# Layer 0: the order of key products, modulation steps and the first w_out loads

## The chip, the cores and the metric

One core of a Trainium2 chip runs the whole kernel. The metric is the device time of one execution in microseconds. The time before is 2219.7 us, the median of three runs (2218.09 to 2219.76).

## The reference, cut to what matters

A two-layer encoder trunk on 256 tokens of width 2048. Each layer computes six modulation vectors from a condition vector `c`, one input projection for four parallel mixers, one output projection, and a gated feed-forward network with a short convolution.

```python
for l in range(DEPTH):                                   # 2 layers
    mod = (c_act @ w_mod[l] + b_mod[l]).reshape(bn, 6, d)   # shift, scale, gate, twice
    h = layer_norm(x) * (1.0 + scale_m) + shift_m
    uv, q_c, kv_c, k_r, sb, sc, sh, ag = jnp.split(h @ w_in[l], IN_SPLITS, axis=-1)
    y_a = gmlp_mixer(uv, ...)
    y_b = mla_mixer(q_c, kv_c, k_r, ...)                  # latent attention with rotary key
    y_c = short_conv_mixer(sb, sc, sh, sconv_w[l])        # sb * conv3(sc * sh)
    y_d = conformer_conv(ag, ...)                         # 31 taps, layer norm, silu
    y = jnp.concatenate([y_a, y_b, y_c, y_d], axis=-1) @ w_out[l]
    x = layer_norm(ALPHA * x + (1.0 + gate_m) * y, ...)
    ...                                                   # shift_f, scale_f, gate_f: conv_ffn
```

In `mla_mixer` the key latent `kv_c` (256 columns) is RMS-normalised and scaled by a gain; the rotary key `k_r` (64 columns) is `k_r * cos + rotated(k_r) * sin`. All of this is float32.

## The kernel before, in words

The weights are larger than the on-chip memory, so they stream through it, issued by SyncE's queue (SP) in program order. A *unit* is one load of a group's weights and the products on it: for a width of 1024 columns, two blocks of 128 rows. `stream` loads a unit, then emits the products of the unit before it, then `pump`s modulation steps at the rate of the phase, then some background steps (the conformer's taps among them).

In layer 0 the weights of w_in are multiplied as they are, in float32 (tile `wexact`, 512 KB per block of 128 rows and 1024 columns; L374). Those tiles take turns through two sets of four buffers. Most other weights go through `wraw` (1 MB; L379) and are split into two halves: ScalarE casts `whi` (L390), VectorE subtracts for `wlo` (L391). In w_out of layer 0 the first two units (`PLAIN_UNITS`) of the first 1024 columns are exact, the next six are split, and the last 1024 columns are exact.

The modulation runs on VectorE beside all of this. Each step takes a 1 MB load (`wmod`) into one of four `raw` buffers and makes one pass of 128x2048 over it. For a gate (`gate_steps`, L295, L205) sixteen steps add up in one accumulator, `macc`, and a bias row follows (L298, L301). For a shift or scale (`column_steps`, `mod_block`, L193, L194) each step gives one column. `mods` is the stream of all these steps, and `next(mods, None)` emits one.

Layer 0 runs its groups in the order of `by_blocks`: the products that need only the first blocks, then the latent group B (`B_w`, `B_n`), whose result starts attention, then the short conv's group C (1024 columns, eight units, two of them loaded ahead), and then w_out.

When B's products are done, `mix_b` loads the attention weights, emits `MODS_AHEAD` = 3 modulation steps and remembers the last of them in `stepped`. It copies the latents out of PSUM (`lat`), and `attend` goes on:

- TensorE transposes the latents into `ps_q` and `ps_kv` (`turn`, L1073); these PSUM tiles (`ms_tile`) are two buffers that all of attention shares, so each new one waits until the one before the last has been read.
- ScalarE scales the query latents (`qg`, L1079, L1082).
- VectorE makes the key's products with cos and sin (`kc`, L1085, L1086) and scales the key latents (`kvr`, L1090). `behind` puts L1085 and L1090 after the step in `stepped` on VectorE's queue. That is an order at build time, without a semaphore.
- TensorE multiplies `kc` by two constant matrices (`ps_kr`), and ScalarE copies the result into `rope` (L1098, L1099). The conformer's scaled taps on ScalarE (`scaled`, L876) stand behind these copies; VectorE adds each tap to `convD` (L879).
- TensorE makes `ps_qn`, `ps_qr`, `ps_kn`, `ps_v` from the latents and the attention weights, and so on to the softmax and its products.

The order of instructions on each engine is fixed when the program is built, by a list scheduler: an instruction that comes earlier in the program goes first, and a later one fills in where the earlier is expected to wait.

Of the kernel before, what the change touches and what calls it, by code (L numbers as in the profile page):

```python
# [9 lines left out]
AF = mybir.ActivationFunctionType  # L10
ALU = mybir.AluOpType
# [4 lines left out]
S = 256  # L16
# [9 lines left out]
C_UV, C_Q, C_SB, C_SC, C_AG = 0, 1024, 1728, 2240, 3264  # L26
# [13 lines left out]
STEPS = [  # L40
    dict(B=1, C=6, out=2, up=2),
    dict(U=7, B=4, C=4, E=8, out=0, up=2),
]

PLAIN_UNITS = 2

MODS_AHEAD = 3

BATCHES = ((0, 4), (4, 4), (8, 4), (12, 4))

# [36 lines left out]
def encoder_kernel(ctx: ExitStack, tc: tile.TileContext, A: dict, consts: bass.AP, out: bass.AP):  # L87
    nc = tc.nc
    pe, act, dve, pool = nc.tensor, nc.scalar, nc.vector, nc.gpsimd
# [41 lines left out]
    sinT = cst[:, 768:1024]  # L131
# [50 lines left out]


    MOD = {}
    last_step = [None]
    data_dep = mybir.DependencyInfo(mybir.DependencyClass.Sync, mybir.DependencyReason.DATA)
    order_dep = mybir.DependencyInfo(mybir.DependencyClass.NoSync, mybir.DependencyReason.DATA)

# [11 lines left out]
    def mod_step(acc, w, kt, first):  # L200
        col = cact[:, kt : kt + 1]
        if first:
            i = dve.tensor_scalar(out=acc, in0=w, scalar1=col, scalar2=None, op0=ALU.mult)
        else:
            i = dve.scalar_tensor_tensor(out=acc, in0=w, scalar=col, in1=acc, op0=ALU.mult, op1=ALU.add)  # L205
        held(i, "mod")
        last_step[0] = i.ins.name

    def gate_rows(l, m, acc):

# [115 lines left out]


    pending = []
    postponed = []
    background = []  # L330

# [28 lines left out]
    def weights(w, k0, nk, c0, width, exact=False, spare=0):  # L360

        w, l = w
        n = nk * width
        if exact:
            parts, per = [], min(nk, max(1, 1024 // width))
            for k in range(0, nk, per):
                if spare:
                    r = slot("wexact")
                else:
                    tag = ("whi", "wlo")[exact_turn[0] % 2]  # L370
                    exact_turn[0] += 1
                    r = splitp.tile([P, 1024], F32, tag=tag, name="wexact")
                m = per * width
                nc.sync.dma_start(out=r[:, :m], in_=w.take(m, rows_of(l, k0 + k, per, c0, width)))  # L374
                for j in range(per):
                    parts.append((r[:, j * width : (j + 1) * width], None))
            return parts
        raw = raw_tile("wraw")
        nc.sync.dma_start(out=raw[:, :n], in_=w.take(n, rows_of(l, k0, nk, c0, width)))  # L379
        per = max(1, 1024 // width)  # L380
        parts = []
        for k in range(0, nk, per):
            m = per * width
            if k < spare:
                hi, lo = slot("thi", F32R), slot("tlo", F32R)
            else:
                hi = splitp.tile([P, 1024], F32R, tag="whi", name="whi")
                lo = splitp.tile([P, 1024], F32R, tag="wlo", name="wlo")
            r = raw[:, k * width : k * width + m]
            held(act.copy(hi[:, :m], r), "cast")  # L390
            i = dve.tensor_tensor(out=lo[:, :m], in0=r, in1=hi[:, :m].bitcast(F32), op=ALU.subtract)  # L391
            held(i, "split")
            for j in range(per):
                parts.append((hi[:, j * width : (j + 1) * width], lo[:, j * width : (j + 1) * width]))
        return parts
# [148 lines left out]
        for u in range(KT // 4):  # L544
            pump()

    def run(g, ahead=0):
        units, load, products, end, bg = g
        loaded = []

        def get(u):
            while len(loaded) < min(u + 1 + (ahead if u > 0 else 0), units):
                loaded.append(load(len(loaded)))
            return loaded[u]

        for u in range(units):
            stream(lambda: get(u), lambda item, u=u: products(item, u), bg)
            pending.extend(postponed)
            postponed.clear()
        pending.append(end)  # L560
# [46 lines left out]
    def out_proj(l, stage, w, src, order, gate_of, name, post_g, post_b, before, then, plain=(), bg=0):  # L607
# [112 lines left out]
        for c0, width in CHUNKS:  # L720
            last = c0 + width == D
            nk = 2048 // width
            units = nkt // nk
            state = {"tail": []}

            def load(u, c0=c0, width=width, nk=nk, units=units, last=last):
                item = load_unit(u, c0, width, nk, units, last)
                if last and u == units - 1:
                    gains()
                return item  # L730

            def load_unit(u, c0, width, nk, units, last):
                kt = order[nk * u]
                assert order[nk * u : nk * u + nk] == list(range(kt, kt + nk))
                spare = nk if last and units - 4 <= u < units - 2 else 0
                exact = c0 in plain or (bool(plain) and u < PLAIN_UNITS)
                parts = weights(w, kt, nk, c0, width, exact, spare)
                s4 = src(kt // 4)
                if exact:
                    return parts, [(s4[:, kt % 4 + k, :], None) for k in range(nk)]  # L740
                acts = []
                for k in range(0, nk, 2):
                    pair = kept.get(kt + k)
                    if pair is None:
                        pair = act_pair("a")
                        split(pair, s4[:, kt % 4 + k : kt % 4 + k + 2, :])
                        if nkt == KT:
                            kept[kt + k] = pair
                    for j in range(2):
                        acts.append([h[:, j, :] for h in pair[:2]])  # L750
                return parts, acts

            def unit(item, u, state=state, c0=c0, width=width, nk=nk, last=last, units=units):
                if u == 0:
                    state["ps"] = [
                        [acc_tile(f"{name}_{c0}{t}{i}") for i in range(width // 512)] for t in range(2)
                    ]
                if last and u >= units - 4:
                    state["tail"].append((item, u))
                    return  # L760
                for t in range(2):
                    products(t, item, state["ps"], u, nk)

            if c0 > 0:
                phase(l, f"{stage}_last" if last else f"{stage}_next")
            for u in range(units):
                stream(lambda: load(u), lambda item, u=u, unit=unit: unit(item, u), bg if c0 == 0 else 1)

            def done(state=state, c0=c0, nk=nk, last=last):
                if c0 == 0:  # L770
                    box["gate"] = gate_of()
                for t in range(2):
                    for item, u in state["tail"]:
                        products(t, item, state["ps"], u, nk)
                    if t == 0 and last and before is not None:
                        before()
                if last:
                    drain_background()
                elif c0 == 0:
                    background.append(lambda: None)  # L780
                for t in range(2):
                    for i, p in enumerate(state["ps"][t]):
                        q = c0 // 512 + i
                        if last:
                            finish(t, p, q)
                        else:
                            background.append(lambda t=t, p=p, q=q: finish(t, p, q))
                    if last:
                        norm(t)
                if last:  # L790
                    closed.append(True)

            pending.append(done)


    def mixers(l, w_in, Y, hF=None, first_mod=None, quarter=None):
# [265 lines left out]
        def attend(WQ, WKV, lat, q01, rr):  # L1062
# [3 lines left out]
            def behind(i):  # L1066
                if stepped:
                    tc.add_manual_dep(i.ins, stepped[0], order_dep, reason="these steps' weights land before the latents turn")
# [14 lines left out]
            by = turn(ps, S, [lat[t][:, 256:320] for t in range(2)])  # L1083
            kc = tmp_tile("kc")
            behind(dve.tensor_tensor(out=kc[0:64, 0:S], in0=by[0:64, :], in1=cosT[0:64, :], op=ALU.mult))  # L1085
            dve.tensor_tensor(out=kc[0:64, S : 2 * S], in0=by[0:64, :], in1=sinT[0:64, :], op=ALU.mult)  # L1086
            ps = ms_tile("ps_kv")
            for j in range(2):
                by = turn(ps, j * S, [lat[t][:, j * P : (j + 1) * P] for t in range(2)])
                behind(dve.tensor_scalar(out=kvr[:, j, :], in0=by, scalar1=KVG(j), scalar2=None, op0=ALU.mult))  # L1090

            rope = slot("rope").rearrange("p (j s) -> p j s", j=4)
            ps = ms_tile("ps_kr")
# [211 lines left out]
    def by_blocks(l, w_in, hF, first_mod, quarter, mix_d, mix_u, gelu_v, mix_v, mix_b, mix_c, mix_e):  # L1305
# [94 lines left out]
            mix_c(cps, tps)  # L1400
            mix_e(sumE, None)

        run(group(w_in, C_SC, 1024, f"C{l}", mix_ce, hF=hf, bg=STEPS[l]["C"]), 2)


    def ffn_up(l, G):
# [280 lines left out]
```

## Time and profile before

| | before |
|---|---|
| median of three runs | 2219.7 us |
| profiled execution, its own time | 2218.06 us |
| its span, first to last instruction | 2216.3 us |
| TensorE busy | 2192.1 us (99%) |
| VectorE busy | 1716.9 us (77%) |
| ScalarE busy | 1092.7 us (49%) |
| DMA, mean over the span | 273 GB/s |

The profile gives, for one execution, the busy time of each engine, groups of instructions by line, and timelines. In a timeline row stand the start in microseconds from the span's beginning, the time taken, the engine, the line of the kernel, the operation, the tile written and the tiles read, the shape and the count of merged instructions, and in brackets the idle time just before and what ended it. SPq is SyncE's queue, where a row is the issue of a transfer. In a row of a stretch stand its bounds, its length, the busy time and count of each engine, the granted TensorE clock, the busy share of the DMA engines and GB/s.

### The profile page before, as it was taken

The page shows a single profiled execution, that of the slowest core. Times are in us where ns is not written, and L with a number is a line of the kernel's source. Part 1 is how long each engine was busy: PE and PEld are TensorE (multiplying, and loading weights), DVE is VectorE, ACT ScalarE, POOL GpSimd, SP SyncE. Part 2 cuts the span into 40 slices and gives each one's busy share as a digit, 9 for nine tenths or more (in the row PEclk, how much of TensorE's full clock was granted, in tenths as well). Part 3 has the DMA queues.
Part 4 walks back from the last instruction along what each step waited for, and adds up shares of the span by engine and source line. Part 5 has one row for each costly group of instructions (what it writes and reads, how often), then busy time and mean ns, then how long its engine had stood idle before and what let it go on. Part 6 is the DMA issues. An engine that isn't in the chain of part 4 may idle for free. (4 is left out here: it accounts for less than half of the span.)

```text
span 2216.3 us, 28397 instructions
## 1 busy us (share of the span) xinstructions
PE 2192.1 (99%) x10880; PEld 1801.1 (81%) x10880; DVE 1716.9 (77%) x2209; ACT 1092.7 (49%) x1677; POOL 21.9 (1%) x38
## 2 busy tenths in 40 slices
PE   9999999999999999999999999999999999999997
PEld 6776875588888888888867988868888888888886
DVE  5658996799888888989968988877766656565776
ACT  3132740655555545545665555465455545454453
POOL 0000000000000000000000000000000000000000
PEclk9999999999999999999999999999999999999999
DMA  9999889588888888888758547856755555555553
GB/s 393 417 374 390 338 330 391 224 331 316 327 315 322 325 328 316 319 329 323 282 208 297 186 156 263 320 197 247 265 210 188 182 198 190 190 190 190 192 192 148
DMA packets 94034, 603.96 MB, mean 273 GB/s; under 512 B 10565, under 2 KB 10693, under 8 KB 29125
## 3 DMA queue, kind: packets, MB, share of 16 engines
q1 hardware_dynamic: 93898, 602.15, 74.0%
q8 instruction: 85, 1.39, 0.2%
q14 instruction: 51, 0.42, 0.1%
HBM read 600.01 MB, written 2.10 MB: 272 GB/s over the span
## 5 line engine op out<-in xcount | busy, mean ns | idle before, releaser
L390 ACT CAST whi<-wraw 128x1024 fp32r<-128x1024 f32 (+1 forms) x608 | 634.5, 1047 | 677.0 <-PE g_c L115 207.8
L391 DVE TENSOR_TENSOR wlo<-wraw,whi 128x1024 fp32r<-128x1024 f32 (+1 forms) x608 | 729.7, 1212 | 285.6 <-ACT whi L390 279.7
L115 PE MATMUL v_c<-hT,whi 128*128 128x512 f32 x1408 | 489.6, 391 | 0.0
L115 PE MATMUL g_c<-hT,whi 128*128 128x512 f32 x1280 | 444.7, 391 | 0.0
L115 PE MATMUL v_c<-hT,wlo 128*128 128x256 f32 x1408 | 394.4, 280 | 0.0
L115 PE MATMUL d<-whi,a 128*128 128x512 f32 x1344 | 386.2, 389 | 0.0
L115 PE MATMUL g_c<-hT,wlo 128*128 128x256 f32 x1280 | 358.4, 280 | 0.0
L194 DVE SCALAR_TENSOR_TENSOR wmod<-wmod,crep 128x2048 f32<-128x2048 f32 x128 | 292.1, 2285 | 45.2 <-DMA wmod<-in_w_mod_dram 44.5
L115 PEld LDWEIGHTS v_c<-hT,whi 128*128 128x128 f32 x1408 | 263.3, 187 | 57.6
L115 PEld LDWEIGHTS d<-whi,a 128*128 128x128 f32 x1344 | 252.2, 188 | 52.2
L115 PEld LDWEIGHTS g_c<-hT,whi 128*128 128x128 f32 x1280 | 239.4, 187 | 52.5
L115 PEld LDWEIGHTS v_c<-hT,wlo 128*128 128x128 f32 x1408 | 266.1, 189 | 0.2
L115 PEld LDWEIGHTS g_c<-hT,wlo 128*128 128x128 f32 x1280 | 241.9, 189 | 0.1
L115 PE MATMUL d<-wlo,a 128*128 128x512 f32 x672 | 232.9, 389 | 0.0
L205 DVE SCALAR_TENSOR_TENSOR macc<-wmod,cact,macc 128x2048 f32<-128x2048 f32 x60 | 140.7, 2346 | 16.1 <-DMA wmod<-in_w_mod_dram 15.7
L115 PEld LDWEIGHTS d<-wlo,a 128*128 128x128 f32 x672 | 126.1, 188 | 26.3
L115 PE MATMUL o<-whi,a 128*128 128x512 f32 x320 | 90.5, 390 | 0.0
L410 DVE TENSOR_TENSOR a<-g,a 128x512 fp32r<-128x512 f32 x132 | 88.6, 682 | 0.0
L534 PE MATMUL first<-wexact,hN 128*128 128x512 f32 x192 | 85.3, 595 | 1.3 <-ACT hN L118 1.0
L409 ACT CAST a<-g 128x512 fp32r<-128x512 f32 x132 | 81.1, 615 | 7.4 <-PE d L115 4.8
L1448 DVE SCALAR_TENSOR_TENSOR u<-g,par,u 128x254 f32<-128x254 f32 (+1 forms) x176 | 74.2, 476 | 0.4 <-ACT u L118 0.2
L115 PEld LDWEIGHTS o<-whi,a 128*128 128x128 f32 x320 | 59.9, 188 | 12.8 <-ACT whi L390 0.4
(321 smaller groups left out, 2379.9 us busy)
## 6 DMA issues: line engine op xcount, KB each, us to landing
wmod<-in_w_mod_dram SPq DMA_DIRECT2D x192, 1024.0 KB, 6.9
wraw<-in_ffn_w_up_dram SPq DMA_DIRECT2D x168, 1024.0 KB, 5.0
wraw<-in_ffn_w_down_dram SPq DMA_DIRECT2D x88, 1024.0 KB, 5.0
wexact<-in_w_in_dram SPq DMA_DIRECT2D x64, 512.0 KB, 9.9
wraw<-in_w_in_dram SPq DMA_DIRECT2D x24, 1024.0 KB, 5.2
wraw<-in_w_out_dram SPq DMA_DIRECT2D x22, 1024.0 KB, 6.3
wexact<-in_w_out_dram SPq DMA_DIRECT2D x20, 512.0 KB, 12.3
wexact<-in_ffn_w_up_dram SPq DMA_DIRECT2D x16, 512.0 KB, 6.5
```

The costliest lines, as they stand in the source:

```text
L115: pe.matmul(o, lhsT, rhs, start=start, stop=stop, skip_group_check=True)
L194: i = dve.scalar_tensor_tensor(out=raw, in0=raw, scalar=1.0, in1=crep, op0=ALU.mult, op1=ALU.mult, accum_out=col)
L205: i = dve.scalar_tensor_tensor(out=acc, in0=w, scalar=col, in1=acc, op0=ALU.mult, op1=ALU.add)
L390: held(act.copy(hi[:, :m], r), "cast")
L391: i = dve.tensor_tensor(out=lo[:, :m], in0=r, in1=hi[:, :m].bitcast(F32), op=ALU.subtract)
L409: act.copy(hi, src)
L410: dve.tensor_tensor(out=lo, in0=src, in1=hi.bitcast(F32), op=ALU.subtract)
L534: i = pe.matmul(ps, hN[kt // 4][:, kt % 4, t * P : (t + 1) * P], parts[kt], start=kt == 0, stop=kt == KT - 1, skip_group_check=True,)
L1448: dve.scalar_tensor_tensor(out=u[:, sh:], in0=x[:, : S - sh], scalar=col(k, j), in1=u[:, sh:], op0=ALU.mult, op1=ALU.add)
```

## The change

It has three parts, all in layer 0.

- `MODS_AHEAD` is 2 instead of 3, and one modulation step is emitted after the key's second product (`kc` with sin); an order at build time keeps that step behind the product on VectorE.
- The two scalings of the key latents (`kvr`) run on ScalarE instead of VectorE, without the order behind `stepped`. (Layer 1 keeps them on VectorE.)
- The weights of w_out's first two units, four transfers of 512 KB, are issued when the short conv's last two units begin, ahead of the modulation steps pumped there, and are used when w_out's units begin.

```diff
-MODS_AHEAD = 3
+MODS_AHEAD = 2
...
-        last_step[0] = i.ins.name
+        last_step[0], last_made[0] = i.ins.name, i
...
-    def run(g, ahead=0):
+    def run(g, ahead=0, next_loads=()):
         units, load, products, end, bg = g
         loaded = []
 
         def get(u):
             while len(loaded) < min(u + 1 + (ahead if u > 0 else 0), units):
                 loaded.append(load(len(loaded)))
+            if u - units + len(next_loads) >= 0:
+                next_loads[u - units]()
             return loaded[u]
...
-                parts = weights(w, kt, nk, c0, width, exact, spare)
+                parts = ready_out.pop(0) if ready_out else weights(w, kt, nk, c0, width, exact, spare)
...
             behind(dve.tensor_tensor(out=kc[0:64, 0:S], in0=by[0:64, :], in1=cosT[0:64, :], op=ALU.mult))
-            dve.tensor_tensor(out=kc[0:64, S : 2 * S], in0=by[0:64, :], in1=sinT[0:64, :], op=ALU.mult)
+            i = dve.tensor_tensor(out=kc[0:64, S : 2 * S], in0=by[0:64, :], in1=sinT[0:64, :], op=ALU.mult)
+            if hF is not None:
+                next(mods, None)
+                tc.add_manual_dep(last_made[0].ins, i.ins.name, order_dep, reason="the key's products come first")
             ps = ms_tile("ps_kv")
             for j in range(2):
                 by = turn(ps, j * S, [lat[t][:, j * P : (j + 1) * P] for t in range(2)])
-                behind(dve.tensor_scalar(out=kvr[:, j, :], in0=by, scalar1=KVG(j), scalar2=None, op0=ALU.mult))
+                if hF is not None:
+                    act.activation(out=kvr[:, j, :], in_=by, func=AF.Copy, scale=KVG(j))
+                else:
+                    dve.tensor_scalar(out=kvr[:, j, :], in0=by, scalar1=KVG(j), scalar2=None, op0=ALU.mult)
...
-        run(group(w_in, C_SC, 1024, f"C{l}", mix_ce, hF=hf, bg=STEPS[l]["C"]), 2)
+        w_out = (A["w_out"], l)
+        out_first = [lambda u=u: ready_out.append(weights(w_out, 2 * u, 2, 0, 1024, True)) for u in range(PLAIN_UNITS)]
+        run(group(w_in, C_SC, 1024, f"C{l}", mix_ce, hF=hf, bg=STEPS[l]["C"]), 2, out_first)
```

More of the change, by code (lines that the diff above doesn't have):

```diff
@@ L184, in encoder_kernel @@
     MOD = {}
-    last_step = [None]
+    last_step, last_made = [None], [None]
     data_dep = mybir.DependencyInfo(mybir.DependencyClass.Sync, mybir.DependencyReason.DATA)
@@ L328, in encoder_kernel @@
     pending = []
+    ready_out = []
     postponed = []
```

## The prediction, before the result was known

> **What bounds the kernel now.** I read the page first, then the busy times by stretch around the changed code, then the timelines of VectorE, TensorE, ScalarE and the DMA issues there, in that order.
>
> ```profile
> span 2216.3 us, 28397 instructions
> PE 2192.1 (99%) x10880; PEld 1801.1 (81%) x10880; DVE 1716.9 (77%) x2209; ACT 1092.7 (49%) x1677; POOL 21.9 (1%) x38
> ```
>
> TensorE is busy for 2192.1 of 2216.3 us, so 24.2 us of idle time is all that removed waits can give back, unless busy time itself is slower than it need be. The page's averages hide that another engine is full in just the stretch that the change touches:
>
> ```profile
> 225.00:240.00 15.00, 15.00 (x67) 10.99 (x66) 14.94 (x15) 15.00 (x38) 0.00 (x0) 1.00 0.58 203
> 240.00:290.00 50.00, 50.00 (x236) 42.59 (x236) 49.05 (x65) 27.16 (x69) 0.00 (x0) 1.00 0.92 346
> 290.00:313.00 23.00, 22.94 (x83) 14.02 (x81) 23.00 (x34) 7.24 (x12) 0.00 (x0) 1.00 0.92 361
> 313.00:325.00 12.00, 11.97 (x51) 9.61 (x52) 10.50 (x15) 5.68 (x6) 0.70 (x1) 1.00 0.96 376
> 325.00:346.00 21.00, 20.94 (x93) 17.02 (x92) 20.26 (x22) 8.53 (x12) 0.00 (x0) 1.00 0.85 322
> 346.00:402.00 56.00, 56.00 (x137) 25.26 (x136) 34.31 (x58) 7.34 (x18) 1.55 (x2) 1.00 0.95 385
> ```
>
> The columns after the length are PE, PEld, DVE, ACT and POOL. From 225 to 313 us TensorE (87.94 of 88) and VectorE (86.99 of 88) are both full; from 346 on VectorE has room (34.31 of 56) and TensorE alone is full. So time gained before 225 reaches the end only as far as VectorE gains it too, up to where its room begins.
>
> The place that is changed, on VectorE:
>
> ```profile
> 205.23 7.32 DVE L205 SCALAR_TENSOR_TENSOR macc<-wmod,cact,macc 128x2048 f32<-128x2048 f32 x3 [8.20 <-DMA wmod<-in_w_mod_dram]
> 212.46 0.41 DVE L1085 TENSOR_TENSOR kc<-ps_q,cst 64x256 f32<-64x256 f32 x1
> 212.80 0.41 DVE L1086 TENSOR_TENSOR kc<-ps_q,cst 64x256 f32<-64x256 f32 x1
> 213.13 0.47 DVE L1090 TENSOR_SCALAR kvr<-ps_kv,par 128x256 f32<-128x256 f32 x1
> 213.52 2.33 DVE L205 SCALAR_TENSOR_TENSOR macc<-wmod,cact,macc 128x2048 f32<-128x2048 f32 x1
> 215.78 0.47 DVE L1090 TENSOR_SCALAR kvr<-ps_kv,par 128x256 f32<-128x256 f32 x1
> 216.17 2.33 DVE L205 SCALAR_TENSOR_TENSOR macc<-wmod,cact,macc 128x2048 f32<-128x2048 f32 x1
> 218.43 1.18 DVE L879 TENSOR_TENSOR convD<-convD,scaled 128x992 f32<-128x992 f32 x1
> 221.70 1.19 DVE L879 TENSOR_TENSOR convD<-convD,scaled 128x988 f32<-128x988 f32 x1 [2.09 <-ACT scaled L876]
> 223.26 1.18 DVE L879 TENSOR_TENSOR convD<-convD,scaled 128x984 f32<-128x984 f32 x1 [0.37 <-ACT scaled L876]
> ```
>
> and on TensorE and ScalarE:
>
> ```profile
> 210.50 0.77 PE L1073 MATMUL ps_q<-cst,lat 128*128 128x128 f32 x4 [0.35 <-ACT qg L1079]
> 211.50 0.44 PE L1073 MATMUL ps_kv<-cst,lat 128*128 128x128 f32 x2 [0.23 <-ACT qg L1079]
> 213.35 0.67 PE L115 MATMUL ps_kr<-kc,cst 64*128 64x256 f32 x2 [1.41 <-DVE kc L1086]
> 213.95 0.44 PE L1073 MATMUL ps_kv<-cst,lat 128*128 128x128 f32 x2
> 216.31 6.93 PE L115 MATMUL ps_qn<-qg,wq 128*128 128x256 f32 x24 [1.29 <-DVE kvr L1090]
> 223.07 1.46 PE L115 MATMUL ps_qr<-qg,wq 128*128 128x256 f32 x6
> 224.37 1.46 PE L115 MATMUL C_c<-hF,wexact 128*128 128x256 f32 x6
> 210.98 0.47 ACT L1079 ACTIVATE qg<-ps_q,par 128x256 f32<-128x256 f32 x1 [0.17 <-PE ps_q L1073]
> 215.05 0.36 ACT L1098 COPY rope<-ps_kr 64x256 f32<-64x256 f32 x1 [3.60 <-PE ps_kr L115]
> 220.68 0.58 ACT L1109 COPY qn<-ps_qn 128x512 f32<-128x512 f32 x1 [2.01 <-PE ps_qn L115]
> ```
>
> Three modulation steps run from 205.23 to 212.55, and only then the key products. The second kvr scaling stands behind a fourth step (213.52 to 215.85), and ps_qn starts at 216.31, when that scaling has given its PSUM tile back. ScalarE is free in between (idle for 3.60 us before 215.05).
>
> **The change, part by part.**
>
> *Key products after two steps.* Two of the three steps take 2 x 7.32/3 = 4.9 us and end at 210.1. Then the products wait for their transposes, the last of the four that start at 210.50 and end at 211.27: they run from 211.3 to 212.05 (0.75 us, as from 212.46 to 213.21), 1.2 us earlier than now. Queued behind the new wait on VectorE is the third step, and with it the fourth and fifth.
>
> *Scalings on ScalarE.* ScalarE's scaling of the same shape from PSUM costs 0.47 us (210.98), VectorE's too (213.13): the price of the move is nothing; between 0.36 (the rope copy) and 0.47 it makes no odds. ScalarE idles there. The first transposes of ps_kv end at 211.94, kvr's first half at 212.45, the second transposes (0.44) at 212.95, its second half at 213.45. The four passes of ps_kr fit beside them from 212.1, when kc has released ps_q's tile. So ps_qn starts at 213.5 instead of 216.31: **2.8 us** earlier on TensorE. The rope copies follow at 213.5, 1.5 us earlier than at 215.05.
>
> *The slow clock behind the wait.* ps_qn's 24 passes take 223.07 - 216.31 = 6.76 us; six passes of the same shape take 224.37 - 223.07 = 1.30, so 24 take 5.2 at full clock. 1.56 us are lost to this:
>
> ```profile
> 209.14:212.55 3.41, 2.23 (x13) 1.19 (x11) 3.28 (x3) 1.31 (x3) 0.00 (x0) 1.00 1.01 423
> 212.55:215.96 3.41, 1.66 (x6) 0.79 (x6) 3.41 (x5) 0.87 (x3) 0.00 (x0) 1.00 1.00 401
> 215.96:219.37 3.41, 3.06 (x7) 2.53 (x8) 3.41 (x3) 2.71 (x7) 0.00 (x0) 0.50 1.02 402
> ```
>
> After 3.41 us in which TensorE was busy for 1.66, the granted clock is 0.50 for the next 3.41 us; after 2.23 busy it was not lowered. With the change the same transposes and key products lie within some 3.8 us instead of 6.6, above 2.23 in 3.41, so I take the slow stretch to go. TensorE then reaches 223.07 at 218.7: **4.4 us** in all.
> The Trainium skill ("TensorE: Matmul & The Clock Gate", Part 1: The HAM clock gate) says that half the clock pulses pass after an idle window of about 3.4 us, and that the window runs free of the kernel, so that what it hits varies from run to run. The length agrees (3.41 us at 0.50); but here a window 49% busy was enough. By the page's idle window, which neither kernel would have here, the sum on TensorE would be 2.8 alone.
>
> *What VectorE gains.* From 212.05 it runs the third, fourth and fifth step, 3 x 2.33, to 219.05; the first convD tap starts there, 0.6 later than at 218.43. But the waits of 2.09 and 0.37 before the next two taps go: ScalarE's scalings for them start 1.5 earlier behind the rope copies, and the qn copy among them, which waited for TensorE until 220.68, comes over 3 us earlier. 2.46 - 0.6 = **1.9 us** earlier from the third tap on. Its idle time up to 313 (0.06 + 0.95) and the 1.5 us between 313 and 325 are what it can catch up besides.
>
> *Which of the two counts.* In w_out's third unit, the first whose weights are split:
>
> ```profile
> 311.76 2.35 DVE L391 TENSOR_TENSOR wlo<-wraw,whi 128x1024 fp32r<-128x1024 f32 x2
> 313.03 0.73 PE L115 MATMUL o<-wlo,a 128*128 128x512 f32 x2
> 324.18 2.36 DVE L391 TENSOR_TENSOR wlo<-wraw,whi 128x1024 fp32r<-128x1024 f32 x2 [0.62 <-ACT whi L390]
> 325.46 0.73 PE L115 MATMUL o<-wlo,a 128*128 128x512 f32 x2
> ```
>
> The first split of the third unit ends at 311.76 + 1.18 = 312.94, and TensorE uses it at 313.03; two units on, 325.36 and 325.46. TensorE has 0.1 us of slack there. So its 4.4 shrink to what VectorE has gained: 1.9, up to 1.9 + 1.0 + 1.5 = 4.4 if all of its gaps close. I take 1.9 plus half of the first 1.0, **2.4 us**; what TensorE has beyond that turns into waits for VectorE (at the rope products, qc, or at these splits).
>
> *w_out's first two units.* They go ahead of the last modulation loads of the short conv:
>
> ```profile
> 263.94 7.07 PE L115 MATMUL C_c<-hF,wexact 128*128 128x256 f32 x32
> 271.52 17.41 SPq L193 DMA_DIRECT2D wmod<-in_w_mod_dram  x5
> 289.02 0.86 SPq L374 DMA_DIRECT2D wexact<-in_w_out_dram  x2
> wexact<-in_w_out_dram SPq DMA_DIRECT2D x2, 512.0 KB, 6.4
> 296.79 13.90 PE L115 MATMUL o<-wexact,ya 128*128 128x512 f32 x32
> ```
>
> The first unit's second transfer is issued at 289.5 and lands 6.4 us later, at 295.9, while TensorE asks at 296.79: 0.9 us of cover, and no gain while that holds. If TensorE came 2.4 to 4.4 us earlier without this move, it would wait for up to 3.5 us, less what VectorE's gain brings the queue forward. With it, the four transfers are issued among the five modulation loads of 271.52 to 288.93, once the short conv's fifth unit has released its buffer (263.94 + 7.07 = 271.0). At about 275 they land at 281, more than 10 us ahead of use. The SP queue carries the same transfers in another order. Passed are three or four loads, which come up to 2 x 0.86 us later into the queue and share 361 GB/s with 1 MB per unit, 2.9 us; VectorE, which uses them, idles 0.95 us in 240 to 290, so they have not been late so far. I cost this at nothing; if that cover is gone, up to 2.9 us per unit.
>
> Sum: the profiled execution took 2218.06 us, 1.8 more than its span. 2218.06 - 2.4 = **2215.7 us**. It lies at the lower end of the runs shown (2218.09 to 2219.76), and their distance of 1.7 is one slow stretch of 3.41 us at half clock. So against the median, 2219.7, the forecast is 4.0 us, 0.18%. What this kernel's measurement can tell from no change is about 0.2%, 4.4 us: faster means under 2215.3, slower over 2224.1.
>
> **Rivals.**
>
> *TensorE's whole gain comes through.* The order on each engine is laid down when the program is built, with lower steps filled in where higher ones are late. w_out's transfers no longer stand ahead of the third unit's, so its split may be placed ahead of a modulation step (2.3 us), and the rope products may be covered by C_c passes, as at 224.37. Then 4.4 us: 2213.7. For it: the third split sits behind such a step. Against: VectorE's total work ahead of the later splits stays the same.
>
> *Nothing is left.* ScalarE, with 0.94 us more to do, starts the taps' scalings no earlier, or the slow stretch stays and holds up the qn copy. Then VectorE keeps its waits and the 0.6 on top: 2218.06 + 0.6 = 2218.7. It also covers the case that w_out's move hides something that was hidden anyway.
>
> *Slower.* Loads that are passed, or whose order is changed, let one more modulation step of 2.28 us slip ahead of a split in w_out's split units. TensorE's slack at the third and fifth is 0.1, so each such step is paid nearly in full: on the 2218.7 without a gain, three units give 2218.7 + 3 x 2.28 = 2225.5. It decides where a split starts later than 311.76 or 324.18. Against: the splits come ahead of their own unit's step in the program.
>
> **How the numbers follow.** VectorE-bound gain 0.48, its own range 2213.7 to 2216.2 (4.4 to 1.9), a third of it under 2215.3; whole gain 0.27, all under 2215.3; nothing left 0.13; slower 0.12. Faster: 0.27 + 0.16 = 0.43. Same: 0.32 + 0.13 = 0.45. Slower: 0.12. The range takes the first three: from 2213.0, the whole gain with 0.7 us for a wait that I priced too low, to 2219.5, nothing left with most of the 1.7 by which runs differ; the slower case and a tail are left out.
>
> **What would show it.** Right: L1085 starts near 211.3, kvr is an ACT instruction, ps_qn starts near 213.5, no 0.50 clock after it; the second tap's wait of 2.09 is gone and convD runs on from 219; the w_out issues stand near 275 and 282; TensorE waits some 2 us in all for qc or wlo between 220 and 330. Wrong: ps_qn still waits past 215; VectorE idles at 210 and again at the taps; a modulation step newly ahead of a split and a PE wait over 1 us at it.

## The result, and the profile after

The changed kernel takes 2226.27 us, the median of seven runs (2225.11 to 2227.95), against 2219.58 us for the kernel before (seven runs, 2218.09 to 2222.0). The ratio is 1.0031, with a 95% interval of [1.0021, 1.004]: slower by 0.31%. The forecast was 2215.7 us, and 2213.0 to 2219.5 as the range. The profiled execution took 2226.12 us with a span of 2224.3 us, where the one before took 2218.06 and 2216.3: 8.06 us more, and that difference is what the rows below have to add up to. (The medians lie 6.69 apart: the profiled execution before was as quick as the quickest of its seven runs.)

At the place of the first two parts, the rows of VectorE, TensorE and ScalarE in the changed kernel's timeline:

```profile
204.78 4.84 DVE L205 SCALAR_TENSOR_TENSOR macc<-wmod,cact,macc 128x2048 f32<-128x2048 f32 x2 [8.02 <-DMA wmod<-in_w_mod_dram]
211.24 0.42 DVE L1088 TENSOR_TENSOR kc<-ps_q,cst 64x256 f32<-64x256 f32 x1 [1.62 <-PE ps_q L1076]
211.91 4.72 DVE L205 SCALAR_TENSOR_TENSOR macc<-wmod,cact,macc 128x2048 f32<-128x2048 f32 x2
217.02 1.19 DVE L882 TENSOR_TENSOR convD<-convD,scaled 128x992 f32<-128x992 f32 x1 [0.38 <-ACT scaled L879]
221.19 1.19 DVE L882 TENSOR_TENSOR convD<-convD,scaled 128x984 f32<-128x984 f32 x1 [1.42 <-ACT scaled L879]
212.84 0.47 ACT L1097 ACTIVATE kvr<-ps_kv,par 128x256 f32<-128x256 f32 x1 [0.53 <-PE ps_kv L1076]
213.37 1.13 PE L115 MATMUL ps_kr<-kc,cst 64*128 64x256 f32 x4 [0.56 <-ACT kvr L1097]
214.43 7.13 PE L115 MATMUL ps_qn<-qg,wq 128*128 128x256 f32 x24
221.40 1.46 PE L115 MATMUL ps_qr<-qg,wq 128*128 128x256 f32 x6
```

The key products start at 211.24, the scalings stand on ScalarE at 0.47 us each, and ps_qn starts at 214.43 where it started at 216.31. These parts do what they say. VectorE idles for 1.62 us ahead of the key products, though, and between them and the first tap it runs two steps (4.72 us) where the forecast had three.

The loss comes later. First the changed kernel's waits of TensorE, with the sum, the number of waits and the longest, then its busy times by stretch (PE, PEld, DVE, ACT, POOL, the clock, the DMA share and GB/s):

```profile
PE o L115 <- ACT whi L391: 6.6, 1, 6.6
PE ps_rD L115 <- DVE dgD L935: 2.0, 2, 1.6
```

```profile
240.00:290.00 50.00, 50.00 (x242) 43.15 (x241) 49.36 (x65) 26.32 (x67) 0.00 (x0) 1.00 0.98 385
290.00:313.00 23.00, 20.86 (x73) 12.15 (x71) 19.66 (x33) 5.66 (x10) 0.70 (x1) 1.00 0.70 253
313.00:325.00 12.00, 5.87 (x16) 4.23 (x17) 11.00 (x15) 6.99 (x10) 0.00 (x0) 0.57 0.73 241
```

Before, the first was not there, and the second was 0.3 us in all. From 290 to 325 TensorE was busy for 34.91 us before and is now busy for 26.73, the last 12 us of it at a clock of 0.57, while the DMA engines, 0.92 and 0.96 busy before, are now 0.70 and 0.73 busy. Up to 290 they are busier than before (0.98 against 0.92 from 240 on). From 290 on the transfers are fewer, not more: something holds them up.

It shows in the changed kernel's timeline around w_out's third unit, the first with split weights (SP's issues, then VectorE, ScalarE and TensorE):

```profile
272.72 3.19 SPq L193 DMA_DIRECT2D wmod<-in_w_mod_dram  x2
276.01 0.90 SPq L375 DMA_DIRECT2D wexact<-in_w_out_dram  x2
282.13 0.33 SPq L193 DMA_DIRECT2D wmod<-in_w_mod_dram  x1
282.55 0.86 SPq L375 DMA_DIRECT2D wexact<-in_w_out_dram  x2
285.35 14.23 SPq L193 DMA_DIRECT2D wmod<-in_w_mod_dram  x4
305.91 0.33 SPq L380 DMA_DIRECT2D wraw<-in_w_out_dram  x1
303.59 2.28 DVE L194 SCALAR_TENSOR_TENSOR wmod<-wmod,crep 128x2048 f32<-128x2048 f32 x1
305.92 0.17 DVE L285 TENSOR_TENSOR mod<-sums,par 128x16 f32<-128x16 f32 x1
319.07 2.36 DVE L392 TENSOR_TENSOR wlo<-wraw,whi 128x1024 fp32r<-128x1024 f32 x2 [1.00 <-ACT whi L391]
314.30 1.58 ACT L948 ACTIVATE yd<-convD,par 128x256 f32<-128x256 f32 x3 [9.26 <-DVE convD L946]
318.01 1.98 ACT L391 CAST whi<-wraw 128x1024 fp32r<-128x1024 f32 x2
308.32 1.84 PE L115 MATMUL ps_var<-ones,sqD 128*128 128x1 f32 x16
311.78 0.70 PE L115 MATMUL ps_rD<-dgD,ones 128*128 128x256 f32 x2 [1.61 <-DVE dgD L935]
319.09 1.22 PE L115 MATMUL o<-whi,a 128*128 128x512 f32 x2 [6.62 <-ACT whi L391]
```

and the rows of the kernel before that answer to these:

```profile
295.94 2.28 DVE L194 SCALAR_TENSOR_TENSOR wmod<-wmod,crep 128x2048 f32<-128x2048 f32 x1
298.26 0.33 SPq L379 DMA_DIRECT2D wraw<-in_w_out_dram  x1
298.55 0.17 DVE L285 TENSOR_TENSOR mod<-sums,par 128x16 f32<-128x16 f32 x1
309.00 1.98 ACT L390 CAST whi<-wraw 128x1024 fp32r<-128x1024 f32 x2
310.52 1.84 PE L115 MATMUL ps_var<-ones,sqD 128*128 128x1 f32 x16
```

TensorE does reach ps_var 2.2 us earlier than before (308.32 against 310.52). But the modulation step that ends at 298.22 before ends at 305.87 now; L285, which closes the shift's sixteen steps, marks this: 298.55 and 305.92. The load of the third unit (`wraw`) goes out 0.04 us after that step ends, in both kernels, for its buffer is one of the four that modulation loads use. It is 7.65 us later, its casts on ScalarE stand behind four `yd` instead of ahead of them, and TensorE waits 6.62 us.

With the waits of 6.62 and 1.61, the 2.2 gained, and some 2.3 us lost (an estimate: half of the 4.57 us for which TensorE was busy at half clock behind the wait, by the rows of the last section), 6.62 + 1.61 + 2.3 - 2.2 = 8.3 us; 8.06 were measured.

### The profile page after: what moved, and what is told of

The parts are those of the page before. It is cut to its first block, busy times and chain, and to the rows that moved or that the text cites. A ratio compares the mean times of both kernels' runs of the same rounds, so it can differ in the third digit from the quotient of the medians.

```text
span 2224.3 us, 28399 instructions
## 1 busy us (share of the span) xinstructions
PE 2193.3 (99%) x10880; PEld 1802.3 (81%) x10880; DVE 1716.6 (77%) x2207; ACT 1094.1 (49%) x1679; POOL 20.0 (1%) x38
```

## The experiments

My theory was that the moved loads of w_out (third part) cost the time, and the first two parts do not. The rival was the fifth modulation step: it is the one whose emission the change moves behind the key product, and so its load goes out behind six loads of the short conv. Four kernels tell these apart. Each ratio is to runs of the kernel before on the same chip, and "L285" is where the shift's steps end in the profiled execution; the last column has the longest wait of TensorE that the kernel before does not have.

| kernel | median us | ratio and interval | L285 | TensorE's new wait |
|---|---|---|---|---|
| before | 2219.58 | | 298.55 | |
| the change | 2226.27 | 1.0031 [1.0021, 1.004] | 305.92 | whi 6.6 |
| e1_no_wout | 2219.82 | 1.0001 [0.9992, 1.001] | 301.31 | wexact 1.9 |
| e2_wout_only | 2224.75 | 1.0022 [1.0013, 1.0031] | 305.81 | dgD 4.1 |
| e3_load_kept | 2226.57 | 1.0033 [1.0022, 1.0045] | 306.19 | whi 6.6 |
| e5_load_kept_no_wout | 2219.57 | 1.0005 [0.9996, 1.0014] | 299.38 | wexact 1.8 |
| e6_cast_first | 2224.74 | 1.0025 [1.0016, 1.0034] | 306.01 | wlo 5.7 |
| e7_split_unit_too | 2225.69 | 1.0028 [1.0016, 1.0039] | 310.14 | whi 5.9 |
| e12_one_unit | 2228.03 | 1.004 [1.0027, 1.0054] | 302.04 | sqD 4.7 |
| e13_kvr_only | 2216.81 | 0.9991 [0.9982, 1.0] | 296.28 | |
| e14_own_queue | 2220.39 | 1.0003 [0.9994, 1.0012] | 300.78 | sqD 1.5 |
| e15_kvr_wout | 2223.68 | 1.0018 [1.0009, 1.0027] | 304.61 | whi 3.4 |
| e16_kvr_own_queue | 2216.45 | 0.9985 [0.9976, 0.9994] | 296.38 | wlo 1.2 |
| e17_key_only | 2219.39 | 1.0 [0.9991, 1.0009] | 298.58 | wexact 1.8 |

**Without the third part (e1).**

```diff
-        run(group(w_in, C_SC, 1024, f"C{l}", mix_ce, hF=hf, bg=STEPS[l]["C"]), 2, out_first)
+        run(group(w_in, C_SC, 1024, f"C{l}", mix_ce, hF=hf, bg=STEPS[l]["C"]), 2)
```

> The changed kernel without its third part: w_out's first two units are issued where they were before. Theory P (the moved w_out loads make the modulation loads, and with them the buffer of the first split unit, late): the wait of 6.6 us for whi and the 1.6 us for dgD vanish, the gain of the first two parts is left, less what TensorE then waits for w_out's first unit: 2215 to 2219 us. Theory Q (the fifth gate step, whose load went behind the six loads of the short conv, sets the whole modulation one step back, and that makes the buffer late): the wait for whi stays, 4 us or more, 2222 to 2226 us.

It takes 2219.82 us, 0.8 above the range for the first theory: the whole loss is gone, and so is the gain. The lead of the first two parts ends at w_out's first unit, whose load goes out at 292.74 (289.02 before), in the waits of TensorE:

```profile
PE o L115 <- DMA wexact<-in_w_out_dram: 1.9, 1, 1.9
```

**The third part alone (e2):** the kernel before, with `ready_out`, `next_loads` and `out_first` of the change.

> The kernel before with only the third part: w_out's first two units are issued with the short conv's last two. Theory P: a wait for whi of 3 to 7 us in w_out's third unit, 2222 to 2228 us. Theory Q: no such wait, 2217 to 2220 us, as before.

It takes 2224.75 us. The moved loads by themselves cost 5.2 us, and here the wait is for the deviation's diagonals, not for the cast.

**The fifth step's load kept in its place (e3, and e5 without the third part).** The load is issued ahead of the short conv's six loads, and the step's instruction stays where the change puts it.

```diff
+            if hF is not None and u == 1:
+                load_early()
...
-            raw = raw_tile("wmod")
-            nc.sync.dma_start(out=raw, in_=A["w_mod"].take(D, rows_of(l, kt, 1, m * D, D)))
+            raw = early.pop() if early else gate_load(l, m, kt)
+            at_step[:] = [l, m, kt]
```

> The changed kernel with all three parts, but the load of the gate step that runs behind the key's products is issued ahead of the short conv's six loads, as before. Theory P: the wait for whi stays within 1 us of 6.6, 2224 to 2228 us. Theory Q: the modulation steps keep their old times, the wait goes, 2214 to 2218 us.

> The changed kernel with that gate step's load kept in its old place and without the moved w_out loads: only the order of the key's products and the scalings on ScalarE are left. Theory P: as without the moved loads, 2215 to 2218 us, up to 2 us better by the step that does not lag. Theory Q: the same as with the load kept alone, 2214 to 2218 us.

Both times stay where they are without this edit (2226.57 and 2226.27; 2219.57 and 2219.82). The rival falls. (e5 lies above both of its ranges; it keeps the wait for `wexact`, 1.8 us.)

**Where in the third unit the time goes (e6, e7).** In e6 the `yd` of ScalarE are ordered behind the first split unit's casts. In e7 that unit's load and split are moved too, together with the two exact units.

```diff
+                    if hF is not None:
+                        tc.add_manual_dep(i.ins, casts[1], order_dep, reason="the first split unit's casts come first")
```

```diff
-        out_first = [lambda u=u: ready_out.append(weights(w_out, 2 * u, 2, 0, 1024, True)) for u in range(PLAIN_UNITS)]
+        unit = lambda u: ready_out.append(weights(w_out, 2 * u, 2, 0, 1024, u < PLAIN_UNITS))
+        out_first = [lambda: unit(0), lambda: (unit(1), unit(2))]
```

> The changed kernel, with the casts of w_out's first split unit ordered ahead of the four yd activations on ScalarE. If the loss is the place in ScalarE's queue (the weights land at 310.7, the cast starts at 318.0), the wait for whi shrinks from 6.6 to under 3 us, the slow-clock stretch behind it with it: 2217 to 2221 us. If the loss is the buffer that comes free late (the load is issued at 305.9 instead of 298.3), TensorE still waits 5 us or more: 2223 to 2227 us.

> The changed kernel, with the load and the split of w_out's third unit (the first split one) moved too, right behind the second unit's load, so that its buffer does not stand behind the last four modulation loads. If the late buffer is the loss, the third unit waits for nothing; TensorE keeps its lead to there, and what the fourth unit waits then decides: 2214 to 2218 us if nothing, 2219 to 2224 us if the late cast only moves to the fourth unit, which still stands behind yd and the modulation steps.

Neither gives the time back (2224.74 and 2225.69 us). The rows show why: in e6 the cast comes at 311.00 instead of 318.01, and the subtraction behind it still waits its turn on VectorE, behind two modulation steps and the `convD` products:

```profile
311.00 1.99 ACT L392 CAST whi<-wraw 128x1024 fp32r<-128x1024 f32 x2 [7.17 <-DMA wraw<-in_w_out_dram]
317.49 2.35 DVE L395 TENSOR_TENSOR wlo<-wraw,whi 128x1024 fp32r<-128x1024 f32 x2
318.76 1.22 PE L115 MATMUL o<-wlo,a 128*128 128x512 f32 x2 [5.72 <-DVE wlo L395]
```

In e7 the third unit runs without a wait, and the fourth waits instead, for its own load and cast:

```profile
309.89 0.72 PE L115 MATMUL o<-whi,a 128*128 128x512 f32 x2
313.82 0.33 SPq L380 DMA_DIRECT2D wraw<-in_w_out_dram  x1
322.01 1.22 PE L115 MATMUL o<-whi,a 128*128 128x512 f32 x2 [5.95 <-ACT whi L391]
```

So no single cast, split or buffer is the cause. Each removal moves the wait to the next piece that stands behind a modulation step.

**Fewer steps ahead of w_out (e8, e9, e10, e11).** The rates at which steps are pumped are lowered in the short conv and raised later. e9 and e11 are the kernel before with the same rates.

```diff
-    C=1.9, out=1.0, out_next=1.55
+    C=1.65, out=1.0, out_next=2.05      # e8, e9
+    C=1.65, out=1.25, out_next=1.75     # e10, e11
```

> The changed kernel with some two modulation steps less pumped in the short conv (rate 1.65 instead of 1.9) and as many more in w_out's second chunk (2.05 instead of 1.55), where VectorE has room. If full VectorE is what turns the moved loads into a loss, the wait for whi goes and TensorE's lead comes through: 2213 to 2217 us. If the order of the loads alone does it, 2221 to 2227 us.

> The control to it: the kernel before with the same two rates. VectorE's lead grows by up to 4.6 us at w_out's split units, where TensorE has waited under 1.2 us in all, so little changes: 2216 to 2219.5 us. If the second chunk or the norm behind it has no room for the two steps, slower by up to their 4.6 us: 2220 to 2224 us.

> The changed kernel with the modulation steps of layer 0 spread otherwise: 1.65 instead of 1.9 a unit in the short conv, 1.25 instead of 1.0 in the first column stretch of w_out, 1.75 instead of 1.55 in the stretches behind it, so that as many steps as before are done by the end of w_out, and two fewer stand in SP's queue ahead of w_out's first split unit. Theory of the freed buffer (the split unit's load waits for a buffer that a modulation step frees, and the moved loads have put that step behind): wraw goes out near 297.6 as in the run with fewer steps, not at 305.9; TensorE's 6.6 us wait for whi and the half clock behind it go; 2216 to 2220 us. Rival (the moved bytes themselves, or the order of the casts on ScalarE, cost the time): TensorE still waits 5 us or more at the third unit, 2223 to 2227 us.

> The control: the kernel before with the same spread of the steps. Theory of the freed buffer: wraw was early enough already, nothing to win there; 2218 to 2222 us, and what the spread costs by itself (a later norm behind w_out) shows here. If this control gains as much as the changed kernel does with the spread, then the spread is a gain of its own and says nothing on the moved loads.

The four take 2227.3, 2227.76, 2227.28 and 2228.35 us (ratios 1.0036, 1.0038, 1.004 and 1.0043, each plus or minus 0.0014 or less). None of the four times lies in a range that I had given. The controls lose as much as the changed kernels: the rates cost some 8 to 10 us by themselves, and beside its controls the change costs nothing more (its share is within their noise). Why the moved loads cost nothing there is not shown, and with losses of this size the times settle nothing about them. One row says more: in e10 I expected `wraw` near 297.6, and

```profile
302.64 0.33 SPq L380 DMA_DIRECT2D wraw<-in_w_out_dram  x1
314.31 1.22 PE L115 MATMUL ps_rD<-dgD,ones 128*128 128x256 f32 x2 [4.13 <-DVE dgD L935]
```

it goes out 5 us later than that, yet 3.3 us earlier than in the changed kernel. The wait for whi goes, and one of 4.13 us for the diagonals takes its place, with a modulation step between the two of them. The theory of one late buffer, which this run was to test, falls with it.

**One unit moved instead of two (e12).** `range(PLAIN_UNITS)` becomes `range(1)`.

> The changed kernel with one unit of w_out moved instead of two. Freed buffer: the step that frees the split unit's buffer stands one place earlier on VectorE (after eight multiplications and two more, but ahead of the centring), so wraw goes out near 303 instead of 305.9; cast near 308; the subtraction still behind the deviation's diagonals, so a wait of 3 to 5 us; 2221 to 2225 us. Rival (moved bytes): half the loss, 2222 to 2224 us, with wraw as late as in the changed kernel. The rows of SP's queue tell them apart, the time hardly.

It takes 2228.03 us, more than with both. Neither expectation held: the `wraw` goes out at 301.80, near what I expected, but the new wait is ps_var's, 4.7 us for `sqD`, since two modulation steps now stand around the centring of `convD` (L910). Behind that wait the second exact unit's 16 passes take 9.69 us, against 7.03 in the changed kernel, with the clock at 0.50 from 306 to 312. That half the bytes cost at least as much speaks against the bytes.

**Place in the queue, or bytes (e14, e16; e13, e15, e17).** What was left was whether the moved loads cost by standing ahead of modulation loads in SP's queue, or by their bytes on the DMA engines. In e14 the change is whole, but GpSimd issues the four moved loads. e16 is the same without the first part. e13 has only the scalings on ScalarE, e15 those and the moved loads on SP, e17 only the key products between the steps.

```diff
-                nc.sync.dma_start(out=r[:, :m], in_=w.take(m, rows_of(l, k0 + k, per, c0, width)))
+                (queue or nc.sync).dma_start(out=r[:, :m], in_=w.take(m, rows_of(l, k0 + k, per, c0, width)))
...
-        out_first = [lambda u=u: ready_out.append(weights(w_out, 2 * u, 2, 0, 1024, True)) for u in range(PLAIN_UNITS)]
+        out_first = [lambda u=u: ready_out.append(weights(w_out, 2 * u, 2, 0, 1024, True, queue=nc.gpsimd)) for u in range(PLAIN_UNITS)]
```

> The changed kernel, with the four moved loads of w_out issued by GpSimd on a queue of its own, so that no modulation load stands behind them in SP's queue; SP then issues seven modulation loads and w_out's first split unit, with nothing between. Theory of the lag (in SP's queue the moved loads push modulation loads back, the modulation steps of VectorE come later by two or three of 2.28 us each, and they then lie between the pieces that w_out's third unit waits for): the shift's last step ends (L285) near 298 to 301 us and not at 305.9; the 6.6 us wait goes; 2216 to 2219.5 us. Rival (the moved bytes, on whatever queue, take the DMA engines from the modulation loads): L285 at 304 us or later, TensorE waits 4 us or more between 305 and 325, 2222.5 to 2227 us.

> The same two parts, the moved loads on GpSimd's queue. Lag: L285 near 296 to 299 us as with the scalings alone; 2214.5 to 2218 us, at best a little below the 2216.8 us of the scalings alone, for w_out's first weights are in early. Rival (moved bytes): L285 at 303 us or later, 2221 us or more.

> The kernel before with the two key-value scalings on ScalarE alone: neither the key products nor any load moved. If the lead that TensorE gets at ps_qn is worth something by itself: ps_qn near 214.5 instead of 216.3, and 2217 to 2218.5 us. If it is lost at w_out's first unit, whose weights then land too late (as in the two runs without the moved loads, 1.8 to 1.9 us): TensorE waits for wexact 1 to 2 us near 297, and 2219 to 2220.5 us.

> The kernel before with the key-value scalings on ScalarE and the two units of w_out moved, the key products left behind three steps. Lag: the moved loads cost as much here as in the whole change and alone, 5 to 7 us, whatever the other parts; L285 near 305 us; 2222.5 to 2226 us. Rival (the loss needs the key products between the steps): 2216.5 to 2219.5 us.

> The kernel before with the key products between the modulation steps alone; scalings on VectorE, no load moved. The two parts together gave nothing (2219.8 us) where the scalings alone gave 2216.8 us. If the key products cost what the scalings win, by the fifth step whose load goes behind the short conv's: L285 near 300 us or later, 2219.5 to 2222.5 us. If they cost nothing by themselves: 2217 to 2219.5 us.

In e14 the loss is gone: 2220.39 us, a little above the range that the lag theory gave, and nowhere near the rival's 2222.5 to 2227. Its issues, and where the shift ends:

```profile
276.17 1.08 POOL L375 DMA_DIRECT2D wexact<-in_w_out_dram  x2 [6.63 <-DMA wexact<-in_w_in_dram]
274.15 23.67 SPq L193 DMA_DIRECT2D wmod<-in_w_mod_dram  x7
300.78 0.17 DVE L285 TENSOR_TENSOR mod<-sums,par 128x16 f32<-128x16 f32 x1
```

The four loads are issued earlier than in the changed kernel (from 268.8 to 278.4 us, against 276.0 to 283.4), and the same bytes move; seven modulation loads follow each other on SP, and the shift ends 5.1 us earlier. The time and L285 are those of the lag theory, but its mechanism is not what the traces show: the passed loads are not pushed back. The shift's last two steps use loads that go out at 282.13 and 285.36 in the changed kernel, each as soon as a step has freed its buffer, and at 283.6 and 286.9 in e14. In the changed kernel they land 6.3 and 8.3 us later, at 288.4 and 293.7, and their steps run only at 296.94 and 303.59 (the second is shown above):

```profile
wmod<-in_w_mod_dram SPq DMA_DIRECT2D x1, 1024.0 KB, 6.3
wmod<-in_w_mod_dram SPq DMA_DIRECT2D x1, 1024.0 KB, 8.3
296.94 2.29 DVE L194 SCALAR_TENSOR_TENSOR wmod<-wmod,crep 128x2048 f32<-128x2048 f32 x1
310.20 0.16 DVE L929 TENSOR_SCALAR rd<-ps_var 128x2 f32<-128x2 f32 x1 [1.90 <-PE ps_var L115]
```

The same two steps in e14:

```profile
295.17 2.28 DVE L194 SCALAR_TENSOR_TENSOR wmod<-wmod,crep 128x2048 f32<-128x2048 f32 x1
298.17 2.28 DVE L194 SCALAR_TENSOR_TENSOR wmod<-wmod,crep 128x2048 f32<-128x2048 f32 x1
```

Up to 292 the changed kernel's steps even run 1.4 us ahead of e14's (290.24 against 291.67). From 292.45 to 303.59 VectorE is busy for 10.62 of 11.14 us, with the first of the two steps and with other work. So the two steps wait for their place in VectorE's order, which is fixed when the program is built, and not for data. e2 and e15 show the same: the two loads have landed by 290.2 and 289.6 us, and the steps run at 296.66 and 303.26, and at 295.25 and 302.06. The row at 310.20 says it once more: VectorE idles there for 1.90 us, with the next step's load issued long before (292.54).

The Trainium skill ("DMA: Bandwidth & Descriptors", Issuing engines are not separate DMA queues) says that issuing from several engines saves only the issuing engine's time, which is usually small. Here the other issuer is worth 5.9 us in the medians, not by the time of an issue but because VectorE's instructions come out in another order.

e16 is the fastest kernel of all, 2216.45 us with a ratio of 0.9985 [0.9976, 0.9994]: it beats the kernel before by 0.15% and, by the medians, the change by 0.44%. e13 comes next, 2216.81 us; its interval reaches 1.0. The moved loads on SP cost 6.0 us on top of e13 (e15: ratios 1.0018 and 0.9991), as they did alone and in the whole change; the loss does not need the other parts. Alone, the key products are worth nothing (e17, 2219.39 us); beside the scalings they cost 2.2 us (e1 against e13, by the ratios, a difference within their intervals) or 3.9 (e14 against e16, by the medians of one set of runs, which is clear of noise). The rows of e13 suggest how:

```profile
204.69 7.33 DVE L205 SCALAR_TENSOR_TENSOR macc<-wmod,cact,macc 128x2048 f32<-128x2048 f32 x3 [8.01 <-DMA wmod<-in_w_mod_dram]
211.93 0.41 DVE L1085 TENSOR_TENSOR kc<-ps_q,cst 64x256 f32<-64x256 f32 x1
214.34 7.13 PE L115 MATMUL ps_qn<-qg,wq 128*128 128x256 f32 x24
```

With three steps ahead of the key products VectorE does not idle, and ps_qn starts as early as in the change (214.34 against 214.43): it is the scalings that held it, not the products. VectorE is then ahead by the 1.62 us that it idles in the change, and by the fifth step, and w_out's first unit is loaded from 286.71 on, early enough that TensorE does not wait for it.

Among the kernels of the table, all with the rates of before, those whose shift ends by 301.31 take at most 2220.39 us, and those whose shift ends at 302.04 or later at least 2223.68. That goes together; e12 shows that L285 alone does not set the loss. What stays open is why the list scheduler lays down the worse order when the four loads stand on SP, and not when they stand on GpSimd: no run shows what it reckons with, and none changed the order alone.

## Why the prediction was wrong, step by step

- *Key products after two steps.* Right in time: 211.24 against a forecast of 211.3. The 1.2 us of VectorE's idle time that this makes (1.62 measured) were in the working, but set off against the waits at the taps. In a stretch where VectorE is full they seem to count: e16, without this part, is 3.9 us faster than e14.
- *Scalings on ScalarE.* Price nothing: right, 0.47 us each, and this is the only part that wins by itself (e13, 0.09%, with an interval that just reaches no gain). The 2.8 us at ps_qn were 1.88, since all four passes of ps_kr came behind the second scaling (213.37) instead of beside it.
- *The slow clock goes.* Wrong; ps_qn still takes 7.13 us. In the rows below TensorE was busy for 2.05 of the 3.41 us ahead of it, between the two values from which I had judged (1.66 and 2.23). So ps_qr came 1.67 us earlier, not 4.4. (In e17 the clock stayed at 1.00 there and ps_qn took 5.45 us, though TensorE was busy for only 1.79 of the 3.41 us ahead of it. So busy time just ahead of ps_qn does not decide by itself, and what does is not shown.)
- *VectorE gains 1.9 us.* The third tap came 2.07 us earlier, as forecast, but with one step fewer done: the fifth step, which I had counted in (three steps from 212.05 to 219.05), was still missing. One step is 2.33 us, so VectorE had gained nothing. e3, which keeps that step's load early, shows that this is not where the loss comes from.
- *Which of the two counts.* The reading was right that w_out's split units had no slack. At ps_var TensorE was 2.2 us ahead; that this is near the 2.4 of the sum is luck, for the 2.4 was to be VectorE's gain, and VectorE had gained nothing.
- *w_out's loads at nothing.* This is the step that failed: the move cost 5.2 us alone (e2) and 6.0 on top of e13 (e15). I argued that the passed modulation loads "have not been late so far", since VectorE hardly idled from 240 to 290, and priced only that they might come late. The issues stand where I had put them (276.01 and 282.55, for 275 and 282), and the passed loads are not late, as the landings above show, nor does VectorE idle now (49.36 of 50 us). What the sum had no term for is the order: with the four loads moved, VectorE runs other work in the steps' place, the sixteenth step ends 7.65 us later, the split unit's load waits for its buffer, and the next steps lie between the pieces that w_out's split units wait for. The price set for lost cover, up to 2.9 us per unit or 5.8 for two, is close to the 5.2 and 6.0 by luck, for it was the price of transfers that land late.
- *The slower rival* was 2225.5 us; the profiled execution took 2226.12. It was right that modulation steps and the third unit's split decide, and that split now starts at 319.07 instead of 311.76. That the number is so near is luck: it let three units pay for one more step each, while in the trace one unit waits, for 1.61 and 6.62 us, with half clock behind. Nor did one more step slip ahead of the split: between L285 and the split there are three, in both kernels. It got 0.12, on the ground that splits come ahead of their own unit's step in the program. That still held (the step at 321.35 comes behind the split); it did not cover the steps of earlier units, which came later themselves.

## What to carry to other kernels

Where the order on each engine is laid down at build time, a load moved forward in one queue can change the order on an engine that only uses the loads it passes. Here the passed loads went out and landed early enough, and the full engine showed no wait for them: it ran the same work in a worse order, and the wait appeared on another engine, later. Before such a load is costed at nothing, build the kernel and follow the passed loads to the work that uses them, and that work to the buffers that it frees and to the pieces that come behind it. If the load must go early, try it from an idle engine, which here kept the order good; and test a change of several parts one part at a time, for here one part won some 2 us, one won nothing and one lost 5 to 6.

## What the runs showed of the hardware

The granted clock of the changed kernel in windows of 3.41 us (columns as above):

```profile
211.07:214.48 3.41, 2.05 (x10) 1.13 (x9) 3.20 (x4) 1.19 (x3) 0.00 (x0) 1.00 1.03 410
214.48:217.89 3.41, 3.41 (x9) 2.79 (x9) 3.03 (x2) 3.32 (x9) 0.00 (x0) 0.50 1.03 406
313.50:316.90 3.40, 0.00 (x0) 0.00 (x0) 3.40 (x6) 2.09 (x4) 0.00 (x0) 0.50 0.59 166
316.90:320.30 3.40, 1.21 (x2) 0.50 (x2) 2.40 (x6) 2.79 (x4) 0.00 (x0) 0.50 0.93 333
320.30:323.70 3.40, 3.36 (x9) 2.68 (x9) 3.40 (x4) 2.11 (x3) 0.00 (x0) 0.50 0.69 198
```

A window with 2.05 us of work (60%) was followed by one at half clock, and behind the long wait the clock stayed at half for one window more, through 3.36 us of work. So the wait was paid a second time here: with the 1.21 us of the window before, TensorE was busy for 4.57 us at half clock, which is about 2.3 us lost on top of the 6.62.
